# One transformer block on one core: the second gate row made in half 0, residual and gates returned in pieces in half 1, four more raw tiles in the f32 stage

## The chip, the cores and the metric

The kernel runs on one core of a Trainium2 chip. The metric is the device time in microseconds (us). The kernel before was timed three times: 2090.99 us in the median, 2086.14 to 2091.57.

## What is computed

One block over 256 tokens of width 2048, all in f32. The condition `c` gives six rows of 2048 through a matrix `ada_w` of 2048 x 12288. Then follow dilated attention, pooling and an output projection, and the part that matters here, a feed-forward over 16384 experts:

```python
def peer_ffn(xn, w_query, sub_keys, w_down, w_up):     # cut to what matters
    s = ...                                            # scores of 8 heads x 2 x 128 keys
    top_s, top_i = lax.top_k(s, 16)                    # 16 experts of each head and token, with gates
    ...
    u = jnp.take(w_down, ic, axis=0)
    a = jax.nn.gelu(jnp.einsum('cd,ced->ce', xc, u)) * gc
    return jnp.einsum('ce,ced->cd', a, jnp.take(w_up, ic, axis=0))

xn2 = rms_norm(h, norm2_g) * (1.0 + scale2) + shift2
h = h + gate2 * peer_ffn(xn2, ...)
return rms_norm(h, final_g)
```

`gate2` is the sixth of the rows that come from `ada_w`: rows 80 to 95 of its 96 blocks of 128.

## The kernel before, in words

The program is one list of steps, run in order. A step reads one block of weights, 128 x 2048 f32 (1 MiB), as two half blocks of 512 KB (`HW` = 1024 columns), and multiplies it on TensorE. For 192 of the 256 tokens the experts are computed densely: all 16384 rows of `w_down` in 128 blocks, then `w_up`, with the gates as a matrix that is zero for experts not chosen. The blocks are taken in two halves of 64 (`HB`): down layer of half 0, up layer of half 0, down layer of half 1, up layer of half 1. For the other 64 tokens the chosen rows are gathered by POOL's indirect DMAs, 1 MiB each, 128 of them in all (`gather`, `sparse_step`); each gathered tile is multiplied on VectorE. How many of these a step gets stands in a list of shares (L1259): 0.95 of one in the f32 stage from its step 24 on, 0.47 in the up layer of half 0, 0.42 and 0.55 in half 1.

The down layer of half 0 is the f32 stage: its matmuls take raw f32 weights and activations. All other layers split each half block into a rounded high part `hi` (ScalarE, L166) and the rest `lo` (VectorE, L172), four tiles of each, and run the matmuls with both. In these layers a step prepares the splits that are needed one and a half steps later.

Loads. SyncE issues all weight loads in one order (`want`, `fill`, L125). A load goes into one of five raw tiles (`RAW_BUFS`); when all are in use, into a `spare` place if there is one. `take` gives out the oldest load, `give` frees its place and issues the next. The list `spare` is filled with three pieces of hT in the up layer of half 0 and late in half 1 (`room`, L1265), as hT isn't needed then. In the f32 stage it is empty.

Work beside the steps. Up to step 19 of the f32 stage a step also loads one half row of `ada_w` and reduces it on VectorE (`ada_half`, L217): these are the 32 halves of gate2's rows. Generators in `side` issue a piece at each half of a step: `route` (choice of experts and gates), `gate_groups` (24 groups of eight tokens: one-hot tiles on VectorE, gate products on TensorE, L1051; the second half's gates are stored to DRAM as `g2d`, 128 x 24 x 64 x 8), and `residual`. A step's `tick` is called once at its end.

For half 1 the gates come back from `g2d` in four tiles `A` of 21, 21, 21 and 1 blocks (`load_gates`, L1015). The first three are 2 MB each in runs of 672 bytes; the fourth, 96 KB, lies in the tail of hT. They are issued in the up layer of half 0 at its steps 22 and 43, and in half 1 at steps 0 and 24. The tensor h, which waits in DRAM as `hsp`, is brought back into hT (2 MB) by one load at step 1 of half 1 (L1275). `residual` (L1214) is started at step 4: POOL adds up rows 80 to 95 of `mod` (`ada_fix`), writes them as one row `g2row` to DRAM in 4-byte elements, and reads it back as `g2b`, broadcast over 128 partitions (L1218, L1220). Two steps later it transposes hT on TensorE (L1228), four 128 x 128 blocks at a time, eight times, and VectorE makes acc = acc x g2b + h (L1231, L1232); for the second token tile ScalarE also copies 64 rows (L1234). POOL also issues all gathers, in the same queue.

Of the kernel before, what the change touches and what calls it, by code (L numbers as in the profile page):

```python
# [10 lines left out]
F32 = mybir.dt.float32  # L11
F32R = mybir.dt.float32r
U32 = mybir.dt.uint32
AF = mybir.ActivationFunctionType
# [3 lines left out]
P = 128  # L18
D = 2048
S = 256  # L20
KC = D // P
# [6 lines left out]
HB = NB // 2  # L28
SP = 64
ND = S - SP  # L30
AB = 21
RS = 24
TG = 8
HW = 1024
RAW_BUFS = 5
HL_BUFS = 4
# [57 lines left out]
def peer_block_kernel(ctx: ExitStack, tc, xT_d, c_d, cols_d, const_d, ada_d, gates_d, wide_d, blk_d, mix_d, br_d,  # L94
                      wout_d, wq_d, keys_d, down_d, up_d, rows_d, fg_d, out_d):
    nc = tc.nc
# [5 lines left out]
    per = ext(tc.tile_pool(name="per", bufs=1))  # L102
    wst = ext(tc.tile_pool(name="wst", bufs=3))
# [16 lines left out]
    spare, next_spare = [], [0]  # L120
# [84 lines left out]
    hT = per.tile([P, KC, S], F32, name="hT")  # L205
    x2f = hT.rearrange("p k s -> p (k s)")[:, :KC * ND].rearrange("p (k n) -> p k n", n=ND)
    cb = per.tile([P, D], F32, tag="cb", name="cb")
# [36 lines left out]


    class Step:
        def __init__(self, src, mm, evac=None, w=D, ada=(), before=(), after=(), tick=None, exact=False):
            self.exact = exact
            self.src, self.mm, self.evac, self.w = src, mm, evac, w
            self.ada, self.before, self.after, self.tick = list(ada), list(before), list(after), tick  # L250
            self.hs, self.ls = [], []
            self.rows = 0

    steps = []
    side, side2, score_q = deque(), deque(), []
# [45 lines left out]
    def run():  # L301
        for n, parts in plan():
            acts = parts[0] + parts[1]
            if n >= 0 and steps[n].exact:
                acts[:0] = [("half", steps[n], i) for i in range(2)]
            for a in acts:
                if a[0] == "ada":
                    want(ada_d[a[1]][:, a[2] * HW:(a[2] + 1) * HW], HW)
                elif a[0] == "half" and (a[2] == 0 or a[1].w == D):
                    w = min(a[1].w, HW)  # L310
                    want(a[1].src[:, a[2] * w:a[2] * w + w], w)
        want(fg_d.unsqueeze(0).to_broadcast([P, D]))
        for n, parts in plan():
            s = steps[n] if n >= 0 else None
            if n >= 1:
                first = parts[0][0] if parts[0] else None
                if first and first[0] == "half" and not (s and s.exact):
                    parts[0][0] = first + (split_hi(first[1], first[2]),)
                if steps[n - 1].evac:
                    steps[n - 1].evac()  # L320
            if s:
                s.mm(s.hs, s.ls, 0)
                side_step(0)
                s.mm(s.hs, s.ls, 1)
                s.hs, s.ls = None, None
            for a in parts[0]:
                act(a)
            while late:
                late.popleft()()
            for _ in range(s.rows if s else 0):  # L330
                sparse_step()
            if s:
                side_step(1)
                if s.tick:
                    s.tick()
            for a in parts[1]:
                act(a)
        if steps[-1].evac:
            steps[-1].evac()
# [157 lines left out]
    n0 = len(steps)  # L497
# [10 lines left out]
    n0 = len(steps)  # L508
# [235 lines left out]
    while gates:  # L744
        steps.append(branch_step(new.popleft() if new[0] <= have and len(new) >= len(old) else old.popleft()))
        if (len(new) + len(old)) % 2 or len(new) + len(old) < 4:
            c, g = gates.popleft()
# [5 lines left out]
    def table(func):  # L753

        t = pp["st"] if "st" in pp else pa.tile([P, 4], F32, tag="st", name="tb")
        nc.scalar.activation(t[:, 0:1], ones[:, 0:1], func)

    hsp = hdram.tile([P, KC, S], F32, name="hsp")
# [28 lines left out]
    w0 = len(steps)  # L787
    for c in range(KC):
        steps.append(block_step(wout_d[c], lambda k: mgd[k // 8][:, k % 8],
                                lambda ps, c=c: wo_done(c, ps)))  # L790
# [9 lines left out]
        while len(order) - len(todo) < seen * len(order) // total:  # L800
            t.ada.append(todo.popleft())

    steps[w0 + 2].tick = lambda: table(AF.Sqrt)

    def fix_mods():
        ada_fix(32, 48)
# [191 lines left out]
    NG = ND // TG  # L998
    half_state = [dict(A=[], evac=0, g=0), dict(A=[], evac=0, g=NG)]

    gdram = ext(tc.tile_pool(name="gdram", bufs=1, space=bass.MemoryType.DRAM))
    g2d = gdram.tile([P, NG, HB, TG], F32, name="g2d")
    NA = -(-HB // AB)

    def get_A(hs, q):
        while len(hs["A"]) <= q:
            n = min(AB, HB - AB * len(hs["A"]))
            if n == AB:
                hs["A"].append(b16([P, NG, n, TG], F32, "A"))
            else:  # L1010
                tail = hT.rearrange("p k s -> p (k s)")[:, KC * ND:KC * ND + NG * n * TG]
                hs["A"].append(tail.rearrange("p (g n u) -> p g n u", n=n, u=TG))
        return hs["A"][q]

    def load_gates(q):  # L1015

        a = get_A(half_state[1], q)
        nc.sync.dma_start(a, g2d[:, :, q * AB:q * AB + a.shape[2], :])

    def gate_groups():  # L1020
        hs = half_state[0]
# [52 lines left out]
    def h_done(half, bl, ps):  # L1074
        hs = half_state[half]
        dst = get_A(hs, bl // AB)[:, :, bl % AB, :]
        n = hs["g"]
        if n:
            hsum = pp["pk2"].tile([P, NG, TG], F32, tag="s1", bufs=S1_BUFS, name="hsum")
            src = hsum  # L1080
            if half:
                both_halves(ps, hsum.rearrange("p g u -> p (g u)"))
            else:
                src = ps[:, :ND].rearrange("p (g u) -> p g u", u=TG)
            nc.scalar.activation(hsum, src, AF.Gelu)  # L1085
            if n < NG:
                nc.scalar.copy(dst[:, n:], hsum[:, n:])
            late.append(lambda: nc.vector.tensor_mul(dst[:, :n], hsum[:, :n], dst[:, :n]))
        else:
            nc.scalar.activation(dst, ps[:, :ND].rearrange("p (g u) -> p g u", u=TG), AF.Gelu)  # L1090
        hs["evac"] = bl + 1

    def open_late():
        pa_ctx.close()
# [102 lines left out]
    fin = {}  # L1197
# [13 lines left out]
            evacuate(fin["acc"][:, 0, c], oc[2 * q], q)  # L1211
            fold(fin["acc"][:SP, 1, c], oc[2 * q + 1])

    def residual():  # L1214

        ada_fix(80, 96)
        row = gdram.tile([KC, P], F32, name="g2row")
        nc.gpsimd.dma_start(row.rearrange("k p -> p k"), mod[:, 80:96])  # L1218
        g2b = fin["g2b"] = per.tile([P, D], F32, tag="cb", name="g2b")
        nc.gpsimd.dma_start(g2b, row.rearrange("k p -> (k p)").unsqueeze(0).to_broadcast([P, D]))  # L1220
        for _ in range(4):
            yield
        for t in range(2):
            for q in range(4):
                acc = fin["acc"][:, t, q * 512:(q + 1) * 512]
                pt = psum("hpt")
                for i in range(4):
                    nc.tensor.transpose(pt[:, i * P:(i + 1) * P], hT[:, 4 * q + i, t * P:(t + 1) * P], ident)  # L1228
                yield
                n = SP if t else P  # L1230
                nc.vector.tensor_mul(acc[:n], acc[:n], g2b[:n, q * 512:(q + 1) * 512])  # L1231
                nc.vector.tensor_add(acc[:n], acc[:n], pt[:n])  # L1232
                if t:
                    nc.scalar.copy(acc[SP:], pt[SP:])  # L1234
                yield

    for half in range(2):
        n0 = len(steps)
        for bl in range(HB):
            steps.append(block_step(down_d[half * HB + bl], x2act if half else lambda k: x2f[:, k, :],  # L1240
                                    lambda ps, half=half, bl=bl: h_done(half, bl, ps), both=half == 1, exact=half == 0))
        if half == 0:
            for m in range(2 * KC):
                steps[n0 - 12 + m].ada.append((80 + m // 2, m % 2))
            steps[n0 + 2].tick = open_late

            steps[n0 + 5].tick = lambda: side.append(gate_groups())
        oc = []
        for bl in range(HB):
            steps.append(up_step(half, bl, oc))  # L1250
            if half == 0 and bl % AB == 1 and bl > AB:
                steps[-1].tick = lambda q=bl // AB - 1: load_gates(q)
        if half == 0:
            steps[-1].evac = lambda oc=oc: keep(oc)
    steps[n0].tick = lambda: load_gates(NA - 2)
    steps[n0 + 24].tick = lambda: load_gates(NA - 1)


    share = [0.95] * (HB - RS) + [0.47] * HB + [0.42] * HB + [0.55] * (HB - 4)  # L1259
    total, seen = sum(share), 0.0  # L1260
    for i, w in enumerate(share):
        n = int(seen / total * 2 * NP + 1e-6)
        seen += w
        steps[n0 - 2 * HB + RS + i].rows = int(seen / total * 2 * NP + 1e-6) - n
    def room(on):  # L1265

        spare.clear()
        if on:
            f = hT.rearrange("p k s -> p (k s)")
            spare.extend(f[:, i * HW:(i + 1) * HW] for i in range(KC * ND // HW))  # L1270

    steps[n0 - HB + 1].tick = lambda: room(True)
    steps[n0 - 8].tick = lambda: room(False)
    steps[n0 + 26].tick = lambda: room(True)
    steps[n0 + 1].tick = lambda: nc.sync.dma_start(hT, hsp)  # L1275
    steps[n0 + 4].tick = lambda: side.append(residual())
    run()


    pk, pk2 = pp["pk"], pp["pk2"]  # L1280
    small = pk.tile([P, 2, 8], F32, name="small")
    acc, g2b = fin["acc"], fin["g2b"]
    fgb = [take() for _ in range(D // HW)]
    nc.scalar.activation(small[:, 0, 7:8], ones[:, 0:1], AF.Sqrt)
    for t in (1, 0):
        for q in range(4):
            c = slice(q * 512, (q + 1) * 512)
            tmp = b16([P, 512], F32, "fin")
            src = oc[2 * q + t]
            if t:  # L1290
                src = fin["rows"][:, c]
# [7 lines left out]
        for q in range(4):  # L1299
            c = slice(q * 512, (q + 1) * 512)  # L1300
# [72 lines left out]
```

## Time and profile before

| what | us |
|---|---|
| median of three runs | 2090.99 |
| the profiled execution's own time | 2092.7 |
| its span | 2090.8 |
| TensorE busy | 1986.3 |
| VectorE busy | 1682.5 |
| ScalarE busy | 904.2 |
| POOL busy | 378.7 |

The span is the time from the first to the last instruction. TensorE is busy for 95% of it, and 65% of the chain that ended last are its instructions; loads are 12% and VectorE 8%. Matmuls overlap, so the sum of their durations says nothing; busy time and counts do.

### The profile page before, as it was taken

To read this page: it belongs to the slowest core of one execution; us is meant where nothing else is said; L and a number is where in the kernel's file an instruction comes from. 1 tells how busy PE (TensorE), PEld (TensorE's weight loads), DVE (VectorE), ACT (ScalarE), POOL (GpSimd) and SP (SyncE) were. 2 spreads that over 40 slices of the span, in tenths; PEclk is the share of its full clock that TensorE was granted. 3 is DMA by queue.
4 is the path that set the end of the run, shared out by engine and by line. 5 is a ranking of instruction groups with operands and counts; after the bars stand their busy time and mean duration, and the time that the engine had idled before them with its cause. 6 is when DMAs were issued, how large, how long until landed. Compare 5 with 4: busy or idle time off the path is not lost.

```text
span 2090.8 us, 33335 instructions
## 1 busy us (share of the span) xinstructions
PE 1986.3 (95%) x12444; PEld 1836.5 (88%) x12444; DVE 1682.5 (80%) x2908; ACT 904.2 (43%) x1473; POOL 378.7 (18%) x384
## 2 busy tenths in 40 slices
PE   6899999999999998999999999998789999999994
PEld 5788999999999998899998888887689999888883
DVE  8987788889888976478886888876678888888886
ACT  3344554544545511012213554544355555545553
POOL 2201231112115700011111010011111112222220
PEclk8999999999999999999999999999799999999997
DMA  9997877788997777699999999989779998999992
GB/s 368 384 342 255 309 266 263 262 286 304 315 327 245 247 244 243 228 355 373 351 353 367 371 330 359 359 333 323 227 264 332 341 334 316 365 348 354 348 349 75
DMA packets 171971, 648.81 MB, mean 310 GB/s; under 512 B 21025, under 2 KB 30529, under 8 KB 155041
## 3 DMA queue, kind: packets, MB, share of 16 engines
q1 hardware_dynamic: 147568, 499.18, 67.3%
q0 software_dynamic: 19200, 136.87, 17.8%
q10 hardware_dynamic: 5042, 10.64, 1.3%
q8 instruction: 98, 1.61, 0.3%
q14 instruction: 63, 0.52, 0.1%
HBM read 636.13 MB, written 10.49 MB: 309 GB/s over the span
## 4 chain that ended last, share of the span: by engine, by line
PE 65%; DMA 12%; DVE 8%; issue 3%; ACT 2%; POOL 0%; DVEq 0%; ACTq 0%; SPq 0%; POOLq 0%
PE oc L1134 11%; PE oc L1132 11%; PE blk L353 10%; PE blk L189 7%; PE oc L1136 6%; DMA raw<-in_ada_dram 4%; PE blk L183 4%; PE blk L184 4%; PE blk L182 4%; PE blk L190 3%; DVE lo L172 2%; DMA raw<-in_wout_dram 2%; DVE raw L219 2%; PE gps L1051 2%; DMA raw<-in_down_dram 2%
## 5 line engine op out<-in xcount | busy, mean ns | idle before, releaser
L172 DVE TENSOR_TENSOR lo<-raw,hi 128x1024 fp32r<-128x1024 f32 (+1 forms) x484 | 575.0, 1196 | 126.1 <-ACT hi L166 122.6
L166 ACT CAST hi<-raw 128x1024 fp32r<-128x1024 f32 (+1 forms) x484 | 491.2, 1021 | 414.6 <-PE oc L1132 128.6
L353 PE MATMUL blk<-hT,raw 128*128 128x192 f32 x2048 | 344.3, 329 | 12.9 <-DMA raw<-in_down_dram 12.9
L353 PEld LDWEIGHTS blk<-hT,raw 128*128 128x128 f32 x2048 | 335.1, 192 | 16.7 <-issue 11.8
L189 PE MATMUL blk<-xn,hi 128*128 128x384 f32 x1024 | 300.0, 365 | 9.5 <-ACT hi L166 8.9
L190 PE MATMUL blk<-xn,lo 128*128 128x192 f32 x1024 | 260.1, 254 | 18.0 <-DVE lo L172 17.9
L219 DVE SCALAR_TENSOR_TENSOR raw<-raw,cb 128x1024 f32<-128x1024 f32 x165 | 213.5, 1312 | 45.9 <-DMA raw<-in_ada_dram 45.3
L1169 POOL DMA_INDIRECT rows<-in_up_dram,spidx x64 | 126.7, 1979 | 512.5 <-DVE rows L1187 253.7
L190 PEld LDWEIGHTS blk<-xn,lo 128*128 128x128 f32 x1024 | 198.9, 194 | 20.7 <-DVE lo L172 20.7
L189 PEld LDWEIGHTS blk<-xn,hi 128*128 128x128 f32 x1024 | 195.6, 191 | 10.8 <-ACT hi L166 9.5
L1132 PE MATMUL oc<-hi,a 128*128 128x512 f32 x512 | 202.6, 396 | 1.7 <-ACT hsum L1085 1.7
L1134 PE MATMUL oc<-hi,a 128*128 128x512 f32 x512 | 202.7, 396 | 0.0
L1134 PE MATMUL oc<-lo,a 128*128 128x512 f32 x512 | 202.5, 396 | 0.0
L1132 PE MATMUL oc<-lo,a 128*128 128x512 f32 x512 | 202.5, 396 | 0.0
L1136 PE MATMUL oc<-hi,a 128*128 128x512 f32 x512 | 202.5, 395 | 0.0
L166 ACT CAST hi<-hT 128x1024 fp32r<-128x1024 f32 x118 | 124.1, 1052 | 122.9 <-PE oc L1132 72.1
L172 DVE TENSOR_TENSOR lo<-hT,hi 128x1024 fp32r<-128x1024 f32 x118 | 142.8, 1223 | 33.6 <-ACT hi L166 30.7
L1180 DVE SCALAR_TENSOR_TENSOR rows<-rows,rows 128x2048 f32<-128x2048 f32 x64 | 146.2, 2284 | 27.9 <-DMA rows<-in_rows_dram,spidx 27.8
L1169 POOL DMA_INDIRECT rows<-in_rows_dram,spidx x64 | 62.7, 980 | 561.5 <-DVE a L1116 233.6
L1187 DVE SCALAR_TENSOR_TENSOR rows<-rows,sph,rows 128x2048 f32<-128x2048 f32 x63 | 147.8, 2345 | 0.8 <-DMA rows<-in_up_dram,spidx 0.8
L182 PE MATMUL blk<-xna,hi 128*128 128x256 f32 x480 | 139.3, 290 | 0.0
L184 PE MATMUL blk<-xna,lo 128*128 128x256 f32 x480 | 136.3, 284 | 0.0
(298 smaller groups left out, 3990.7 us busy)
## 6 DMA issues: line engine op xcount, KB each, us to landing
raw<-in_down_dram SPq DMA_DIRECT2D x229, 512.0 KB, 6.7
raw<-in_ada_dram SPq DMA_DIRECT2D x165, 512.0 KB, 5.7
raw<-in_up_dram SPq DMA_DIRECT2D x165, 512.0 KB, 6.9
hT<-in_up_dram SPq DMA_DIRECT2D x91, 512.0 KB, 7.2
raw<-in_blk_dram SPq DMA_DIRECT2D x80, 512.0 KB, 5.8
raw<-in_wout_dram SPq DMA_DIRECT2D x32, 512.0 KB, 6.1
raw<-in_wq_dram SPq DMA_DIRECT2D x32, 512.0 KB, 5.6
xraw<-in_ada_dram SPq DMA_DIRECT2D x27, 512.0 KB, 6.4
```

Source lines behind the costliest of these rows:

```text
L166: nc.scalar.copy(hi, r)
L172: nc.vector.tensor_sub(lo, r, s.hs[i].bitcast(F32))
L182: nc.tensor.matmul(out, wh, ah, start=start, stop=False)
L184: nc.tensor.matmul(out, wl, ah, start=False, stop=stop)
L189: nc.tensor.matmul(ps[:, :2 * ND], wh, a.rearrange("p s n -> p (s n)"), start=start, stop=False)
L190: nc.tensor.matmul(ps[:, :ND], wl, a[:, 0, :], start=False, stop=stop)
L219: nc.vector.scalar_tensor_tensor(raw, raw, 1.0, cb[:, i * HW:(i + 1) * HW], op0=ALU.mult, op1=ALU.mult, accum_out=modp[:, i, m:m + 1])
L353: nc.tensor.matmul(st["ps"][:, :ND], raw[:, c], a, start=k == 0, stop=k == KC - 1)
L1132: nc.tensor.matmul(o, a[:, P:P + 2 * SP], w, start=st_, stop=sp_)
L1134: nc.tensor.matmul(o, a[:, :P], w, start=st_, stop=sp_)
L1136: nc.tensor.matmul(o, a[:, P + 2 * SP:], w, start=False, stop=False)
L1169: nc.gpsimd.indirect_dma_start(rows[:, j % 2, :], None, table_rows["down" if j < NP else "up"], bass.IndirectOffsetOnAxis(sp["idx"][:, j % ...
```

## The change

- A step may have several ticks; `tick` becomes a list `ticks`.
- `load_gates` spreads a load over four steps, a quarter of the 24 groups in each (one piece for the small fourth tile). The first two begin where they were. The third begins at step 18 of half 1 instead of step 0.
- hT comes back in four loads at steps 2, 4, 6 and 8 instead of one at step 1; `residual` starts at step 10 instead of 4, without its waits and without the gate row.
- `gate_row`, the POOL part of `residual`, is called at step 22 of the f32 stage.
- At step 1 of the f32 stage `spare` is filled with four new tiles of the `hi` ring, which has no splits in it during that stage, and emptied eight steps before the stage's end.

```diff
-    def load_gates(q):
-        a = get_A(half_state[1], q)
-        nc.sync.dma_start(a, g2d[:, :, q * AB:q * AB + a.shape[2], :])
+    def load_gates(n, q, parts=4):
+        def load(g):
+            a = get_A(half_state[1], q)
+            nc.sync.dma_start(a[:, g], g2d[:, g, q * AB:q * AB + a.shape[2], :])
+        for i in range(parts):
+            g = slice(i * NG // parts, (i + 1) * NG // parts)
+            steps[n + i].ticks.append(lambda g=g: load(g))
...
+    def room(where=None):
+        spare.clear()
+        if where == "h":
+            f = hT.rearrange("p k s -> p (k s)")
+            spare.extend(f[:, i * HW:(i + 1) * HW] for i in range(KC * ND // HW))
+        elif where:
+            spare.extend(wst.tile([P, HW], F32, tag="hi", bufs=HL_BUFS, name="spare") for _ in range(HL_BUFS))
...
-    def residual():
+    def gate_row():
         ada_fix(80, 96)
         row = gdram.tile([KC, P], F32, name="g2row")
         nc.gpsimd.dma_start(row.rearrange("k p -> p k"), mod[:, 80:96])
-        g2b = fin["g2b"] = per.tile([P, D], F32, tag="cb", name="g2b")
-        nc.gpsimd.dma_start(g2b, row.rearrange("k p -> (k p)").unsqueeze(0).to_broadcast([P, D]))
-        for _ in range(4):
-            yield
+        fin["g2b"] = per.tile([P, D], F32, tag="cb", name="g2b")
+        nc.gpsimd.dma_start(fin["g2b"], row.rearrange("k p -> (k p)").unsqueeze(0).to_broadcast([P, D]))
+
+    def residual():
+        g2b = fin["g2b"]
+        yield
...
+            steps[n0 + 1].ticks.append(lambda: room("split"))
+            steps[n0 + 22].ticks.append(gate_row)
+            steps[n0 + HB - 8].ticks.append(lambda: room())
...
-    steps[n0].tick = lambda: load_gates(NA - 2)
-    steps[n0 + 24].tick = lambda: load_gates(NA - 1)
+    for q in range(NA - 2):
+        load_gates(n0 - HB + AB * (q + 1) + 1, q)
+    load_gates(n0 + 18, NA - 2)
+    load_gates(n0 + 24, NA - 1, 1)
...
-    steps[n0 + 1].tick = lambda: nc.sync.dma_start(hT, hsp)
-    steps[n0 + 4].tick = lambda: side.append(residual())
+    for q in range(4):
+        steps[n0 + 2 + 2 * q].ticks.append(lambda c=slice(4 * q, 4 * q + 4): nc.sync.dma_start(hT[:, c, :], hsp[:, c, :]))
+    steps[n0 + 10].ticks.append(lambda: side.append(residual()))
```

## Rows read from the trace of the kernel before

**Rows 1.** Windows by stage: length, busy time and count by engine, clock, DMA share, GB/s.

```profile
core 0: us, PE busy (x) PEld busy (x) DVE busy (x) ACT busy (x) POOL busy (x), PEclk, DMA share, GB/s
...
725.00:1131.00 406.00, 392.70 (x2518) 388.54 (x2517) 289.85 (x900) 72.75 (x293) 42.70 (x46) 0.99 0.87 310
1131.00:1432.00 301.00, 298.62 (x1280) 239.79 (x1278) 243.17 (x315) 153.02 (x196) 32.84 (x31) 1.00 0.94 348
1432.00:1763.00 331.00, 304.19 (x2077) 300.64 (x2078) 257.34 (x306) 171.48 (x264) 44.38 (x31) 0.95 0.88 307
```

**Rows 2.** Chain of waits in the f32 stage: start us, us, what.

```profile
926.75 1.78 PE gps L1051 x16
928.54 7.80 PE blk L353 x48
```

**Rows 3.** Windows of the two stretches and of half 1's rest.

```profile
744.00:858.00 114.00, 101.11 (x584) 97.23 (x583) 74.08 (x316) 12.54 (x28) 1.14 (x2) 0.97 0.74 245
...
1432.00:1615.00 183.00, 156.19 (x1036) 152.64 (x1037) 130.67 (x156) 85.29 (x132) 20.79 (x17) 0.92 0.84 284
1615.00:1763.00 148.00, 148.00 (x1043) 148.00 (x1042) 126.67 (x151) 86.19 (x132) 23.59 (x14) 1.00 0.91 335
```

**Rows 4.** Chain of waits, 765 to 810 us.

```profile
776.59 4.38 DMA raw<-in_ada_dram
...
781.00 1.25 DVE raw L219 x2
...
782.26 6.17 DMA raw<-in_ada_dram
```

**Rows 5.** SyncE's waits, 733 to 858 us: us in total, times, longest.

```profile
SPq L141 <- DVE raw L219: 41.8, 8, 6.7
...
SPq L141 <- PE blk L353: 9.0, 7, 2.8
```

**Rows 6.** Timeline of SyncE's issues at the start of half 1.

```profile
1437.81 0.75 SPq L1018 DMA_DIRECT2D A<-g2d  x1
...
1445.76 0.43 SPq L1275 DMA_DIRECT2D hT<-hsp  x1
```

**Rows 7.** ScalarE's waits, 1432 to 1600 us.

```profile
ACT hi L166 <- DMA raw<-in_down_dram: 25.6, 5, 8.0
```

**Rows 8.** Timeline of POOL, 1465 to 1500 us; idle time before in brackets.

```profile
1470.52 1.25 POOL L1218 DMA_DIRECT2D g2row<-mod  x1 [0.29 <-POOL mod L227]
1485.02 0.57 POOL L1220 DMA_DIRECT2D g2b<-g2row  x1 [13.26 <-DMA g2row<-mod]
```

**Rows 9.** VectorE's waits, 1432 to 1600 us.

```profile
DVE acc L1231 <- DMA g2b<-g2row: 17.0, 1, 17.0
```

**Rows 10.** Windows of single stretches of half 1, columns as in rows 1.

```profile
1505.00:1520.00 15.00, 15.00 (x109) 14.78 (x107) 12.97 (x17) 5.99 (x10) 2.31 (x2) 1.00 0.81 266
1442.00:1447.00 5.00, 5.00 (x37) 5.00 (x36) 4.39 (x5) 1.99 (x4) 0.10 (x1) 1.00 1.05 323
...
1448.00:1464.00 16.00, 10.28 (x67) 9.39 (x65) 3.66 (x6) 4.14 (x8) 0.58 (x1) 0.91 1.01 410
...
1475.00:1487.00 12.00, 8.82 (x61) 8.18 (x59) 3.07 (x5) 2.06 (x3) 1.57 (x2) 0.92 0.99 121
```

**Rows 11.** Chain of waits, 893 to 910 us: the first gather.

```profile
883.16 10.42 DMA rows<-in_rows_dram,spidx
```

**Rows 12.** Timeline of VectorE in the residual's second token tile.

```profile
1519.58 1.23 DVE L172 TENSOR_TENSOR lo<-raw,hi 128x1024 fp32r<-128x1024 f32 x1 [1.72 <-ACT hi L166]
...
1522.55 0.68 DVE L1231 TENSOR_TENSOR acc<-acc,g2b 64x512 f32<-64x512 f32 x1
...
1531.87 1.23 DVE L172 TENSOR_TENSOR lo<-raw,hi 128x1024 fp32r<-128x1024 f32 x1 [1.72 <-ACT hi L166]
...
1540.28 1.23 DVE L172 TENSOR_TENSOR lo<-raw,hi 128x1024 fp32r<-128x1024 f32 x1 [1.72 <-ACT hi L166]
```

**Rows 13.** Window around the fourth gate load.

```profile
1600.00:1615.00 15.00, 14.23 (x98) 13.72 (x98) 12.56 (x14) 9.91 (x15) 1.68 (x1) 1.00 1.01 390
```

More of the change, by code (lines that the diff above doesn't have):

```diff
@@ L246, in peer_block_kernel, with __init__ @@
     class Step:
-        def __init__(self, src, mm, evac=None, w=D, ada=(), before=(), after=(), tick=None, exact=False):
+        def __init__(self, src, mm, evac=None, w=D, ada=(), before=(), after=(), exact=False):
             self.exact = exact
             self.src, self.mm, self.evac, self.w = src, mm, evac, w
-            self.ada, self.before, self.after, self.tick = list(ada), list(before), list(after), tick
+            self.ada, self.before, self.after = list(ada), list(before), list(after)
             self.hs, self.ls = [], []
-            self.rows = 0
+            self.rows, self.ticks = 0, []
     steps = []
@@ L333, in run @@
                 side_step(1)
-                if s.tick:
-                    s.tick()
+                for f in s.ticks:
+                    f()
             for a in parts[1]:
@@ L801, in peer_block_kernel @@
             t.ada.append(todo.popleft())
-    steps[w0 + 2].tick = lambda: table(AF.Sqrt)
+    steps[w0 + 2].ticks.append(lambda: table(AF.Sqrt))
     def fix_mods():
@@ L1244, in peer_block_kernel @@
                 steps[n0 - 12 + m].ada.append((80 + m // 2, m % 2))
-            steps[n0 + 2].tick = open_late
-            steps[n0 + 5].tick = lambda: side.append(gate_groups())
+            steps[n0 + 1].ticks.append(lambda: room("split"))
+            steps[n0 + 2].ticks.append(open_late)
+            steps[n0 + 5].ticks.append(lambda: side.append(gate_groups()))
+            steps[n0 + 22].ticks.append(gate_row)
+            steps[n0 + HB - 8].ticks.append(lambda: room())
         oc = []
@@ L1250, in peer_block_kernel @@
             steps.append(up_step(half, bl, oc))
-            if half == 0 and bl % AB == 1 and bl > AB:
-                steps[-1].tick = lambda q=bl // AB - 1: load_gates(q)
         if half == 0:
             steps[-1].evac = lambda oc=oc: keep(oc)
-    steps[n0].tick = lambda: load_gates(NA - 2)
-    steps[n0 + 24].tick = lambda: load_gates(NA - 1)
+    for q in range(NA - 2):
+        load_gates(n0 - HB + AB * (q + 1) + 1, q)
+    load_gates(n0 + 18, NA - 2)
+    load_gates(n0 + 24, NA - 1, 1)
     share = [0.95] * (HB - RS) + [0.47] * HB + [0.42] * HB + [0.55] * (HB - 4)
@@ L1264, in peer_block_kernel @@
         steps[n0 - 2 * HB + RS + i].rows = int(seen / total * 2 * NP + 1e-6) - n
[L1265 to L1274, printed above, removed]
-    steps[n0 + 1].tick = lambda: nc.sync.dma_start(hT, hsp)
-    steps[n0 + 4].tick = lambda: side.append(residual())
+    steps[n0 - HB + 1].ticks.append(lambda: room("h"))
+    steps[n0 - 8].ticks.append(lambda: room())
+    steps[n0 + 26].ticks.append(lambda: room("h"))
+    for q in range(4):
+        steps[n0 + 2 + 2 * q].ticks.append(lambda c=slice(4 * q, 4 * q + 4): nc.sync.dma_start(hT[:, c, :], hsp[:, c, :]))
+    steps[n0 + 10].ticks.append(lambda: side.append(residual()))
     run()
```

## The prediction, made before the changed kernel was run

> **What bounds the kernel now.** I read the stages first. The reader is to see that TensorE is busy all but 2 us of the up layer of half 0 [rows 1]: nothing hidden there is worth anything. The losses lie in the two down layers. A step of either is 32 matmuls. In the f32 stage an undisturbed step is 32 x 7.80/48 = 5.20 us, and after every step and a half 16 small gate products add 1.78 [rows 2]. From 744 to 858 us, its steps 2 to 19, TensorE ran 584 matmuls, 3 of them transposes: 581 x 0.1625 = 94.4 us of work in 114, so 19.3 us were lost [rows 3]. In half 1's down layer the undisturbed rate is 148/1043 = 0.1419 us a matmul, 4.54 us a step. From 1432 to 1615 us there are 1036, of which 32 are the residual's transposes: 1004 x 0.1419 = 142.5 in 183, an excess of 40.5 us [rows 3]. These two stretches are what the change touches; together they are 59.8 us.
>
> Next I read what each stretch waits for. In the first, the chain is load, VectorE, load: an `ada` half row lands in 4.38 to 6.17 us, VectorE multiplies it in 1.25, and only then the next `ada` load starts [rows 4]. SyncE, which issues all loads in order, waited mostly for VectorE there (41.8 us for that multiplication alone) and 9.0 for TensorE [rows 5]: the five raw tiles are shared out so that one goes round among the `ada` rows, and the weight loads stand behind it. In the second stretch two things are seen. The 2 MB of gates and the 2 MB of hT were issued 8 us apart [rows 6], ahead of the weights, and ScalarE waited 25.6 us for raw tiles [rows 7]. Then the gate row: its write to DRAM held POOL 13.26 us before the broadcast could be issued [rows 8], and VectorE stood 17.0 us at the first residual product [rows 9] with the splits queued behind it. In both stretches the granted clock fell (0.97 and 0.92 in the mean, 1.00 beside them [rows 3]), so part of each excess is matmuls at 1.2 GHz after a stall; it goes with the stalls.
>
> **The f32 stage: four more raw tiles.** Nothing is added but 2 MB fetched earlier. Nine loads are three steps, so an `ada` load waits for a multiplication about three steps back and no longer for the last one. The DMA need is 1.5 MiB a step, 1.573 MB; at the 410 GB/s of a saturated stretch [rows 10] that is 3.84 us of 5.20. VectorE's 74.1 us of work in the stretch [rows 3] have to fit in 94.7: they do, at 78%. So I expect steps near 5.2 us from about step 4 on. At best all 19.3 us go; at worst none, if the `ada` chain stays (a rival). I take 17, near the best, since the floor is held right after step 19, where the `ada` loads end. The first two steps keep their loss, because the tiles are opened at the end of step 1.
>
> **The gate row in half 0.** Its POOL work goes from half 1 to step 22 of the f32 stage: two small adds, the row's write 1.25, a wait of 13.26, the broadcast 0.57, some 16 us [rows 8]. POOL had 1.14 us to do in that stretch [rows 3], and its queue doesn't wait for TensorE, so it starts when the last `ada` product (step 19) is made: about 858 - 17 = 841 in the new time, done at 857. Queued behind it are the first two row gathers, then due at 883 - 17 = 866 [rows 11]: 9 us to spare. The row's write also clogs the DMA engines: from 1475 to 1487 they were 0.99 busy and moved 121 GB/s [rows 10]. In the new place there are no `ada` loads any more and nine tiles hold 4.5 steps, 23 us of weights, against 12. I cost it at nothing; without that cover it is the 12 us of the clog or the 13.26 of POOL.
>
> **Gates in quarters in the up layer.** No step there lost anything with 2 MB in one piece [rows 1], so quarters bring and cost nothing.
>
> **The start of half 1.** The gates' 2 MB leave steps 0 to 8; hT comes in four pieces at steps 2, 4, 6, 8; the 17.0 us wait for the row is gone, as the row has been there since half 0. What is late next is the DMA. A step needs 1 MiB of weights (2.56 us at 410 GB/s [rows 10]), 0.42 of a 1 MiB gather (the share in the code; 1.07 us), and half a piece of hT (0.64): 4.27 us of 4.54. It fits, barely. I take 1 us, between 0 and 3.
>
> **The residual at steps 11 to 18.** Its 32 transposes stay: 109 matmuls took 15.00 us, 12 of them transposes [rows 10], so (15.00 - 97 x 0.1419)/12 = 0.10 each, 3.3 us. Its VectorE work is a product of 0.68 us a step [rows 12] and a sum that I take to be as long, and for the second token tile a ScalarE copy waits for VectorE and the splits stand behind that copy. Before, such steps took 6.1 us, and 8.4 with a gathered row (12.29 us for two, 8.41 for the next [rows 12]); 20.70 for three, against 4.96 with transposes. But there VectorE came out of the 17 us wait with no split ready ahead. With splits one and a half steps ahead I expect most of it hidden: 2 us, between 0 and 4 x (6.90 - 4.96) = 7.8.
>
> **The third gate tile at steps 18 to 21.** A quarter runs at 323 GB/s [rows 10], 1.62 us: the step's DMA need is 2.56 + 1.07 + 1.62 = 5.25, 0.7 too much, 2.8 in four steps, partly covered by the raw tiles: 2 us, between 0 and 5.7 (twice 2.8, if the residual has left no lead). Here a rule speaks against the change. The Trainium skill, "DMA: Bandwidth & Descriptors", section "Rules for kernel authors", wants at least 1 MiB per DMA, and its section on the anatomy of one DMA gives a fixed cost of about 2.0 us each. If these costs stood one behind the other, an estimate by that page for the 12 additional DMAs would be 24 us, and the sum would give back half of what it gains. The up layer moved 348 GB/s in loads of 512 KB with its DMA engines 0.94 busy [rows 1]; so the trace does not agree that pieces of this size are slow when others are queued behind them.
>
> The small fourth gate load at step 24 is unchanged; what it costs lies in the last 15 us, 15.00 - 98 x 0.1419 = 1.1 [rows 13].
>
> **The sum.** Half 1: of 40.5, there remain 3.3 + 1.1 + 1 + 2 + 2 = 9.4; 31.1 go. With 17 of the f32 stage 48.1. The profiled execution took 2092.7 us (span 2090.8), so 2044.6; it was 1.7 above the median of the runs shown, so **2043 us** for a median.
>
> **Rivals.**
> 1. The f32 stage gains nothing: raw tiles come round so that each `ada` load still waits for the last multiplication. For it: that is how five tiles behaved, against the number of tiles. Against: the four new tiles go round in a fixed order, three steps apart. 2060.
> 2. Half 1 keeps its pace: VectorE and ScalarE wait for each other in the residual (7.8), hT costs 3, the third gate tile 5.7. For it: the 8.41 us came with ScalarE as the releaser and not a load [rows 12]. There remain 20.9: 2054.5.
> 3. The gate row is late or clogs the loads in the f32 stage: up to 13.3 more, 2056. For it: 9 us to spare is not much.
> 4. Slower: in half 1 steps 2 to 21 the DMA queue saturates with only five raw tiles, and each step takes the 8.41 us of the slowest residual step. 20 x (8.41 - 4.54) = 77.4, and 1.1, in the place of 40.5; with the 17 us of the f32 stage 2091 - 17 + 38 = 2112. It decides when a step's DMA need passes 4.54 us for all twenty; by my working it is 4.27, and 5.25 only in four.
> 5. The pieces cost their whole latency: 12 more DMAs, each holding the loads behind it for 4.38 us as one `ada` load did [rows 4], are 53 us: 2096, no change. Against: the up layer's rate [rows 1]. That is what the rule above would come to here.
>
> **Chances.** Forecast 0.60, rival 1 0.14, rival 2 0.14, rival 3 0.06, rival 4 0.03, rival 5 0.03. The likeliest case alone spans 2036 (both stretches at their best: 19.3 and 36.1) to 2050. The range reaches to rivals 1, 2 and 3, and below by half of the spread of the runs shown: 2033 to 2063. A measurement of this kernel tells 0.3%, 6 us, from no change: faster 0.94, same 0.03, slower 0.03.
>
> **What will show it.** f32 stage: steps 2 to 19 should take 95 to 97 us, VectorE's wait for `ada` loads should shrink and SyncE should wait for TensorE; an unchanged 114 is rival 1. The write of the row should start near 841 us and the gathers not move against their picks; an idle TensorE before the gate products is rival 3. Half 1: no VectorE wait for the row, and 1432 to 1615 shrunk to about 152 us; steps over 6 us from the eleventh to the eighteenth are rival 2, ScalarE waiting for raw tiles from step 2 on is rival 4. The up layers must stay as they are. I am wrong if either stretch gives back less than half.

## The result, and the profile after

The changed kernel took 2041.0 us in the median of four runs (2039.94 to 2044.54); beside it the kernel before took 2091.28. The ratio is 0.976, with a 95% interval of 0.974 to 0.979: some 50 us less. It was run again later on another chip: 2041.9 against 2092.5, ratio 0.9755 (0.974 to 0.977). The forecast was 2043.

The stages of the profiled execution (2039.94 us, span 2038.1), in the columns of [rows 1]:

```profile
726.00:1112.00 386.00, 386.00 (x2522) 385.94 (x2521) 290.17 (x904) 73.47 (x293) 45.45 (x51) 1.00 0.92 328
1112.00:1413.00 301.00, 298.93 (x1281) 240.02 (x1279) 243.81 (x317) 152.67 (x195) 33.75 (x31) 1.00 0.94 348
1413.00:1712.00 299.00, 296.71 (x2082) 295.39 (x2083) 257.85 (x306) 172.67 (x266) 44.70 (x27) 1.00 0.93 338
```

Against [rows 1] the f32 stage went from 406 to 386 us, the up layer stayed at 301, half 1's down layer went from 331 to 299: 52 us, of 52.8 between the two profiled executions (50 between the medians: the one profiled here was the fastest of its four). TensorE is now busy for all of the f32 stage, and the granted clock is 1.00 in all three.

Steps 2 to 19 of the f32 stage, which took 114 us before, and then the same 114 us of the trace as in [rows 3], which now reach into step 23:

```profile
746.00:840.00 94.00, 94.00 (x582) 93.98 (x581) 78.36 (x331) 12.30 (x27) 2.79 (x5) 1.00 0.92 317
744.00:858.00 114.00, 114.00 (x704) 113.98 (x703) 87.42 (x362) 13.62 (x31) 3.34 (x6) 1.00 0.92 302
```

704 matmuls where there were 584, none waiting. The DMA engines are at 0.92 instead of 0.74. What SyncE waits for, 734 to 840 us, has changed sides against [rows 5], and the chain there, which was loads and VectorE [rows 4], is TensorE alone:

```profile
SPq L141 <- PE blk L353: 67.5, 35, 2.8
SPq L141 <- DVE tops L860: 7.7, 2, 6.0
```

```profile
764.92 25.19 PE blk L353 x155
```

POOL's timeline, against [rows 8] and [rows 11]:

```profile
834.36 0.22 POOL L226 TENSOR_TENSOR mod<-modp 128x16 f32<-128x16 f32 x1 [82.46 <-DVE spare L219]
...
835.17 1.21 POOL L1231 DMA_DIRECT2D g2row<-mod  x1 [0.29 <-POOL mod L227]
849.40 0.55 POOL L1233 DMA_DIRECT2D g2b<-g2row  x1 [13.03 <-DMA g2row<-mod]
865.24 1.03 POOL L1183 DMA_INDIRECT rows<-in_rows_dram,spidx  x1 [15.29 <-DVE spidx L1176]
```

The write still holds POOL 13.03 us, but the first gather comes 15 us after the broadcast and waits for its own indices, not for POOL's queue. The clog is still there too and costs nothing: from 835 to 850 the DMA engines are 0.90 busy with 164 GB/s, and TensorE runs through. In half 1, the start with hT's pieces, the residual, and the stretch with the last two gate tiles:

```profile
835.00:850.00 15.00, 15.00 (x94) 15.00 (x93) 13.40 (x42) 0.82 (x3) 1.76 (x2) 1.00 0.90 164
1423.00:1460.00 37.00, 37.00 (x263) 37.00 (x262) 30.66 (x35) 21.73 (x33) 5.03 (x3) 1.00 0.97 368
1460.00:1500.00 40.00, 40.00 (x289) 40.00 (x289) 37.40 (x47) 20.96 (x34) 6.71 (x4) 1.00 0.82 295
1500.00:1560.00 60.00, 58.18 (x403) 56.91 (x401) 50.53 (x62) 34.20 (x53) 8.39 (x5) 1.00 0.99 355
1600.00:1700.00 100.00, 100.00 (x705) 100.00 (x705) 84.30 (x98) 58.11 (x89) 15.45 (x9) 1.00 0.90 326
```

Under hT's pieces the DMA engines are 0.97 busy and TensorE loses nothing. Only the fourth line loses: 60.00 - 403 x 0.1419 = 2.8 us. VectorE, which stood 17.0 us for the gate row [rows 9], doesn't wait for it any more. Its waits in steps 0 to 38 are short ones, nearly all for ScalarE's copies of sums:

```profile
DVE hsum L195 <- ACT hsum L194: 19.2, 17, 2.3
```

### The profile page after: what moved, and what is told of

Same layout as the page of the kernel before. It is cut to its first block, busy times and chain, and to the rows that moved or that the text cites. A ratio compares the mean times of both kernels' runs of the same rounds, so it can differ in the third digit from the quotient of the medians.

```text
span 2038.1 us, 33369 instructions
## 1 busy us (share of the span) xinstructions
PE 1973.6 (97%) x12444; PEld 1828.1 (90%) x12444; DVE 1683.2 (83%) x2908; ACT 905.6 (44%) x1473; POOL 387.6 (19%) x384
## 4 chain that ended last, share of the span: by engine, by line
PE 74%; DVE 7%; DMA 6%; ACT 2%; issue 2%; DVEq 0%; ACTq 0%; POOL 0%
PE blk L353 16%; PE oc L1146 12%; PE oc L1148 12%; PE blk L189 8%; PE oc L1150 6%; PE blk L183 4%; PE blk L182 4%; PE blk L184 4%; PE blk L190 4%; DVE lo L172 2%; DMA raw<-in_wout_dram 2%; DMA raw<-in_blk_dram 2%; PE gps L1056 2%; DVE raw L219 1%; ACT hi L166 1%
## 5 line engine op out<-in xcount | busy, mean ns | idle before, releaser
L189 PE MATMUL blk<-xn,hi 128*128 128x384 f32 x1024 | 293.2, 360 | 0.7 <-ACT acc L551 0.7
L1183 POOL DMA_INDIRECT rows<-in_up_dram,spidx x64 | 141.4, 2209 | 480.7 <-DVE rows L1201 241.7
L353 PE MATMUL blk<-hT,raw 128*128 128x192 f32 x1280 | 212.3, 326 | 0.0
L353 PEld LDWEIGHTS blk<-hT,raw 128*128 128x128 f32 x1280 | 207.7, 190 | 0.0
L219 DVE SCALAR_TENSOR_TENSOR raw<-raw,cb 128x1024 f32<-128x1024 f32 x153 | 197.5, 1311 | 9.5 <-DMA raw<-in_ada_dram 9.5
```

The lines of the kernel that those rows point to most:

```text
L189: nc.tensor.matmul(ps[:, :2 * ND], wh, a.rearrange("p s n -> p (s n)"), start=start, stop=False)
L219: nc.vector.scalar_tensor_tensor(raw, raw, 1.0, cb[:, i * HW:(i + 1) * HW], op0=ALU.mult, op1=ALU.mult, accum_out=modp[:, i, m:m + 1])
L353: nc.tensor.matmul(st["ps"][:, :ND], raw[:, c], a, start=k == 0, stop=k == KC - 1)
L1183: nc.gpsimd.indirect_dma_start(rows[:, j % 2, :], None, table_rows["down" if j < NP else "up"], bass.IndirectOffsetOnAxis(sp["idx"][:, j % ...
```

## The experiments

Each kernel is the changed one with one part altered, or the kernel before with one part of the change. Times are medians beside runs of the kernel before on the same chip; "lost" is the length of a stretch less its matmuls at 0.1625 us (f32 stage) or 0.1419 (half 1) and less 0.1 us for each transpose, where any are taken off. The "clog" is the stretch in which the row's write is under way and the DMA engines move little; the "lead" is what splits are ready ahead of TensorE. In these traces the f32 stage's first matmul starts between 729.5 and 735.7 us, though no edit touches what runs before it; so differences of a few us between kernels are better read from the windows than from the medians.

**1. Without the four extra raw tiles.**

```diff
-            steps[n0 + 1].ticks.append(lambda: room("split"))
```

> The changed kernel without the four extra raw tiles in the f32 stage (five tiles throughout it), all else kept. Theory: those tiles alone took the 19.3 us out of steps 2 to 19, so about 19 us come back: 2060. The gate row's write now falls on five tiles instead of nine: where I costed it at nothing under the cover of nine tiles, up to 12 us more should show as TensorE waiting for weight loads in steps 20 to 23: 2060 to 2072, I expect about 2065. Rival: the gain of the f32 stage came from elsewhere (the load order, the moved row): 2041 to 2045.

2062.8 us, ratio 0.986 (0.984 to 0.988): 22 us of the gain gone. The window of steps 2 to 19 and of the gate row's write, and SyncE's waits before 858 us:

```profile
745.00:859.00 114.00, 103.50 (x613) 100.36 (x612) 79.99 (x335) 12.65 (x28) 2.79 (x5) 0.99 0.79 258
859.00:877.00 18.00, 15.82 (x97) 15.35 (x96) 7.49 (x24) 0.99 (x3) 0.55 (x1) 1.00 0.98 218
```

```profile
SPq L141 <- DVE raw L219: 36.4, 8, 7.1
...
SPq L141 <- PE blk L353: 16.1, 14, 2.8
```

SyncE waits for VectorE again, 114.0 - 0.3 - 610 x 0.1625 = 14.6 us are lost, and the clog costs 18.0 - 97 x 0.1625 = 2.2 more: far from 12. Of the 19.5 us between the profiled executions of this kernel and the changed one, the other 3 or so are in half 1, which ran at the slower of two rhythms (last section). So the time came out near the expected one, but the stretch itself gave back 14.6 us and not 19: with five tiles its loss was 19.3 before, 14.6 here and 17.0 in experiment 5, and why it varies isn't shown. The rival falls.

**2. One extra tile instead of four**, to tell the `ada` chain from the depth of the queue.

```diff
-            spare.extend(wst.tile([P, HW], F32, tag="hi", bufs=HL_BUFS, name="spare") for _ in range(HL_BUFS))
+            spare.extend(wst.tile([P, HW], F32, tag="hi", bufs=HL_BUFS, name="spare") for _ in range(1))
```

> The changed kernel with one extra raw tile in the f32 stage instead of four (six tiles), all else kept. Chain theory: the five tiles let each ada load wait for the ada product just before it; with six, the ada rows alternate between the sixth tile and others, so a load waits for a product two steps back, and most of the 19 us stays gained: at most 5 us are lost again, 2041 to 2046, and SyncE waits for TensorE, not for VectorE. Depth theory (the rival): what counts is how many loads are ahead, each tile giving its share: one of four keeps a quarter, so 12 to 15 us come back: 2053 to 2058.

2043.7 us, ratio 0.978 (0.975 to 0.981). Steps 2 to 19, and the row's write behind them; SyncE's waits, 734 to 850 us; and three `ada` loads with two of the products:

```profile
741.00:835.00 94.00, 94.00 (x581) 93.98 (x580) 74.48 (x319) 12.21 (x27) 2.40 (x5) 1.00 0.90 303
835.00:860.00 25.00, 22.72 (x130) 22.45 (x129) 12.45 (x39) 1.32 (x4) 0.93 (x2) 0.93 0.88 242
```

```profile
SPq L141 <- PE blk L353: 61.4, 32, 4.8
SPq L141 <- DVE raw L219: 9.1, 4, 4.3
```

```profile
746.49 0.33 SPq L141 DMA_DIRECT2D raw<-in_ada_dram  x1
...
752.07 0.42 SPq L141 DMA_DIRECT2D spare<-in_ada_dram  x1
...
756.89 0.33 SPq L141 DMA_DIRECT2D raw<-in_ada_dram  x1
```

```profile
754.61 1.21 DVE L219 SCALAR_TENSOR_TENSOR raw<-raw,cb 128x1024 f32<-128x1024 f32 x1
...
759.72 1.22 DVE L219 SCALAR_TENSOR_TENSOR spare<-spare,cb 128x1024 f32<-128x1024 f32 x1
```

The 581 matmuls of [rows 3] take 94.00 us with six tiles as with nine (582 in the changed kernel, 581 in experiment 3). The `ada` rows alternate between a raw tile and the sixth: the load at 756.89 goes out 2.8 us before the product of the row ahead of it begins, where with five tiles it started as that product ended [rows 4]. So one tile more, which parts successive `ada` rows, takes all of that loss away: the chain theory holds, and depth at so much a tile does not. The other three tiles matter behind it: with six, the clog costs 25.0 - 130 x 0.1625 = 3.9 us.

**3. The four tiles alone, in the kernel before.**

```diff
+    def split_room():
+        spare.extend(wst.tile([P, HW], F32, tag="hi", bufs=HL_BUFS, name="spare") for _ in range(HL_BUFS))
...
+            steps[n0 + 1].tick = split_room
...
+            steps[n0 + HB - 8].tick = spare.clear
```

> The kernel before with the four extra raw tiles in the f32 stage and nothing else. Theory: it gains what its removal cost by the matmul count of steps 2 to 19, 18 to 20 us: 2071 to 2073, with half 1 as it was (its steps 4 to 16 with some 40 us of excess). Rival: faster arrival at half 1 or other buffers change half 1 too: outside 2068 to 2076.

2076.0 us, ratio 0.993 (0.990 to 0.995), at the edge of the rival's bound. The trace says why:

```profile
743.00:837.00 94.00, 94.00 (x581) 93.82 (x580) 78.29 (x331) 12.21 (x27) 1.14 (x2) 1.00 0.92 318
```

```profile
1431.00:1614.00 183.00, 156.37 (x1034) 153.16 (x1033) 132.34 (x158) 86.73 (x134) 22.21 (x17) 0.92 0.85 287
1614.00:1742.00 128.00, 128.00 (x885) 128.00 (x884) 107.54 (x126) 72.79 (x111) 20.20 (x12) 1.00 0.89 324
```

All of the f32 stage's loss is gone, and half 1's first 183 us are as in [rows 3] (1034 matmuls, 1036 before). But the rest of half 1 ran at 128/885 = 0.1446 us a matmul instead of 0.1419, 2.4 us here, of which the last section tells.

**4. The gate row made in half 1 again.**

```diff
-            steps[n0 + 22].ticks.append(gate_row)
...
     def residual():
+        gate_row()
         g2b = fin["g2b"]
-        yield
+        for _ in range(4):
+            yield
```

> The changed kernel with the gate row made again at the start of the residual in half 1 (step 10 there, transposes four half steps later, as before), all else kept. Theory: the row's clog of the DMA engines and VectorE's wait for the broadcast are the larger part of half 1's gain: VectorE again waits 10 to 17 us at the first residual product and 15 to 22 us come back: 2056 to 2063. Rival: the wait of 17 us was itself a consequence of the two 2 MB loads, which delayed the row; with these in pieces the row's chain takes its 13 + 10 us mostly beside other work: 2041 to 2047.

2059.9 us, ratio 0.984 (0.982 to 0.986): 19 us back, with hT and the gates in pieces. VectorE's wait, POOL's wait for the row, and the window from there to the residual's end:

```profile
DVE acc L1249 <- DMA g2b<-g2row: 7.1, 1, 7.1
```

```profile
1480.29 0.57 POOL L1233 DMA_DIRECT2D g2b<-g2row  x1 [13.30 <-DMA g2row<-mod]
```

```profile
1474.00:1546.00 72.00, 59.46 (x387) 57.28 (x387) 50.95 (x64) 31.57 (x49) 6.70 (x6) 0.93 0.86 267
```

The time came as expected, the wait did not: 7.1 us instead of 10 to 17. So the rival was right in part: from write to arrival the row took 24 us in both kernels, but in the kernel before VectorE stood at it for 10 us longer. Lost are 72.0 - 3.3 - 355 x 0.1419 = 18.3 us, so more than half of it lies outside that wait, in the clog and in the steps after the wait, which have no lead; the two weren't told apart.

**5. The row early, alone, in the kernel before.**

```diff
-    def residual():
+    def gate_row():
...
+    def residual():
+
+        g2b = fin["g2b"]
...
+            steps[n0 + 22].tick = gate_row
```

`gate_row` is what `residual` did ahead of its yields.

> The kernel before with the gate row made at step 22 of the f32 stage and nothing else; residual still starts at step 4 of half 1, hT and the third gate tile still come in one load each at steps 1 and 0. Theory: VectorE's 17 us wait goes and with it the slow residual steps behind it; the 4 MB of loads still cost their 10 us; the row's clog under five raw tiles costs about 3 in the f32 stage: 2068 to 2076. Rival: with the row there early VectorE waits in the same place for something else (the gathers, the raw tiles behind the 4 MB), and half of the 17 us stays: 2078 to 2086.

2081.5 us, ratio 0.996 (0.994 to 0.998): 11 us, a miss, within the rival's bounds. The 4 MB of loads, then the residual:

```profile
1454.00:1477.00 23.00, 16.62 (x98) 15.74 (x98) 13.09 (x17) 10.06 (x16) 1.68 (x1) 0.85 0.85 329
...
1502.00:1541.00 39.00, 33.34 (x207) 32.10 (x207) 31.44 (x38) 19.13 (x29) 3.95 (x3) 0.91 0.71 237
859.00:879.00 20.00, 17.32 (x97) 17.05 (x96) 12.25 (x38) 0.80 (x4) 0.75 (x2) 0.91 0.94 223
```

VectorE doesn't wait for the row any more, but 23.0 - 98 x 0.1419 = 9.1 us are lost to the loads, and the residual, close behind, goes at the slow pace of [rows 12]: 39.0 - 207 x 0.1419 = 9.6 us, 12 transposes included. The likely reason is that the loads use up the lead. The clog on five tiles costs 4.2 in the f32 stage. So the parts aren't additive: the row's 19 us are to be had in full only with the loads out of the residual's way and more tiles under the row.

**6. hT and the third gate tile early and whole again.**

```diff
-    load_gates(n0 + 18, NA - 2)
+    load_gates(n0, NA - 2, 1)
...
-    for q in range(4):
-        steps[n0 + 2 + 2 * q].ticks.append(...)
+    steps[n0 + 1].ticks.append(lambda: nc.sync.dma_start(hT, hsp))
```

> The changed kernel with the third gate tile in one load at step 0 and hT in one load at step 1 of half 1, as before, the gate row still in half 0 and the residual still at step 10. Theory: the 4 MB ahead of five raw tiles cost steps 4 to 8 what they cost before, 8 to 12 us: 2049 to 2053. Rival: with no row and no residual close behind them the loads are made up by the lead of the splits: 2041 to 2044.

2051.6 us, ratio 0.981 (0.979 to 0.983). The window of these loads, and ScalarE's wait for raw tiles in half 1 (16.0 us in the changed kernel, 5.2 of them before 1500 us, where TensorE lost nothing):

```profile
1422.00:1455.00 33.00, 26.47 (x164) 25.67 (x164) 20.64 (x24) 12.94 (x21) 5.03 (x3) 0.90 0.91 347
```

```profile
ACT hi L166 <- DMA raw<-in_down_dram: 31.3, 13, 7.7
```

33.0 - 164 x 0.1419 = 9.7 us lost, as in the theory; the rival falls. From step 21 on this trace, too, has the slower rhythm of the last section.

**7. The new places, but whole loads.**

```diff
-    def load_gates(n, q, parts=4):
+    def load_gates(n, q, parts=1):
...
-    for q in range(4):
-        steps[n0 + 2 + 2 * q].ticks.append(...)
+    steps[n0 + 2].ticks.append(lambda: nc.sync.dma_start(hT, hsp))
```

> The changed kernel with each of the three 2 MB gate loads and hT in one piece, at the places where their pieces begin now (up layer steps 22 and 43; half 1 step 18 for gates, step 2 for hT). Theory: where eight tiles are there (the up layer) nothing changes; in half 1 each 2 MB load ahead of five raw tiles stalls TensorE for 3 to 6 us, so 2046 to 2053. By the rule that pieces cost a fixed time each it would be faster than with pieces: below 2041.

2043.9 us, ratio 0.9765 (0.9745 to 0.978): a miss on the low side, by its median not told from the changed kernel. hT's 2 MB in one load at step 2 stalled nothing (steps 2 to 10 took 4.55 us each); the last two gate tiles did. Both together, then the third alone:

```profile
1501.00:1553.00 52.00, 48.36 (x321) 47.14 (x320) 39.35 (x47) 26.58 (x43) 6.72 (x4) 0.97 0.94 325
1514.00:1530.00 16.00, 14.03 (x86) 13.55 (x86) 11.77 (x13) 8.77 (x14) 1.68 (x1) 0.89 0.88 318
```

52.0 - 321 x 0.1419 = 6.5 us, 3.8 of it for the third tile, against 2.8 for both tiles with the third in quarters (5.5 in the second trace of the changed kernel). So 2 MB in one load cost nothing for hT and 3.8 us for a gate tile, and the two issued 8 us apart ahead of five tiles cost 9 to 10. It isn't the size alone; but the gate tile by itself at step 0 wasn't run, so how much of the 10 us is its own stays open. Nor is the reverse true: whole loads are not faster.

**8. The last two gate tiles later still.** Twice; the second time beside the changed kernel on one chip.

```diff
-    load_gates(n0 + 18, NA - 2)
-    load_gates(n0 + 24, NA - 1, 1)
+    load_gates(n0 + 24, NA - 2)
+    load_gates(n0 + 32, NA - 1)
...
-    steps[n0 + 26].ticks.append(lambda: room("h"))
+    steps[n0 + 20].ticks.append(lambda: room("h"))
```

> The changed kernel with hT's three extra raw tiles opened at step 20 of half 1 instead of 26, the third gate tile in quarters at steps 24 to 27 instead of 18 to 21, and the small fourth tile in quarters at steps 32 to 35 instead of whole at 24. The changed kernel still loses about 3.3 us over its step of 4.55 at steps 19, 20, 25, 29 and 30. Theory: with eight raw tiles these loads are covered as in the up layer: up to 3 us faster, 2038 to 2041. Rival: the small runs of 32 bytes cost the DMA engines the same wherever they stand: 2041.

> The changed kernel itself once more, beside the next one on one chip. Both theories: 2041.

> The kernel with the last two gate tiles later, under eight raw tiles, again. Theory: the 3.3 us of stalls at steps 19, 20, 25, 29 and 30 are what it gains, 2.5 of them in the trace: 2036 to 2039, its runs below those of the changed kernel on the same chip. Rival: the 4.6 us between the medians came from different chips and from the part of the program before the change: 2040 to 2042.

2036.4 us, ratio 0.975 (0.972 to 0.977); then 2036.5, ratio 0.974 (0.972 to 0.975), where the changed kernel took 2041.9. On the shared chip its five runs were 2034.9 to 2040.4, those of the changed kernel 2039.1 to 2042.8. The two windows, of this kernel and then of the changed one, from the last pair:

```profile
1500.00:1560.00 60.00, 59.01 (x414) 58.50 (x413) 54.53 (x65) 35.90 (x56) 9.52 (x6) 1.00 0.99 370
1560.00:1700.00 140.00, 140.00 (x987) 140.00 (x986) 118.15 (x137) 81.52 (x124) 20.81 (x14) 1.00 0.93 338
```

```profile
1500.00:1560.00 60.00, 56.15 (x384) 54.62 (x383) 49.33 (x58) 32.99 (x52) 8.39 (x5) 1.00 0.98 348
1560.00:1700.00 140.00, 140.00 (x967) 140.00 (x967) 117.78 (x136) 79.45 (x122) 21.89 (x13) 1.00 0.90 330
```

1.3 us lost in the first 60 where the changed kernel lost 5.5, and 20 matmuls more in the next 140 us, 2.8 us. The first is what the theory said; the second is the slower rhythm of the last section, which this trace of the changed kernel has, its first trace doesn't, and neither trace of this kernel does. It is the version with the lowest median; the intervals of the two ratios overlap and so do the runs, the medians on the shared chip are 5.4 us apart, and the windows account for 7. Three things moved at once (the tiles opened earlier, the third gate tile later, the fourth later and in quarters), and which of them does it wasn't told apart.

## Why the prediction was right

- **f32 stage, 17 us.** The stage shrank by 20. The mechanism held as put: the `ada` chain through one tile (experiments 1 and 2), with more tiles than it needs, since one parts the rows. VectorE's wait for `ada` loads fell from 42.6 us to 18.6, as the signs asked. The term was sized too small: all of the 19.3 went, and some 0.7 of step 27 that I had not counted.
- **Gate row in half 0 at no cost.** It held; the write began at 835 us (841 forecast), the first gather at 865 (866). The price without cover was put too high: 12 us by the clog's length, 2.2 to 4.2 with five tiles and 3.9 with six, since even these hold part of it.
- **Quarters in the up layer.** Nothing, as said.
- **hT in pieces, 1 us.** Nothing was lost. The DMA need of 4.27 us of 4.54 is 0.94, and 0.97 busy was measured; but the pieces weren't needed, as one piece at the same place did as well (7). The sign of rival 4, ScalarE waiting for raw tiles, did show (16.0 us), without reaching TensorE under hT's pieces.
- **Residual, 3.3 for transposes and 2.** 289 matmuls took 40.00 us; with 28 transposes, 261 x 0.1419 = 37.0, so 0.11 a transpose (0.10 forecast), and nothing else lost. That the splits' lead hides this work fits the two runs in which a stall just before had used it up and the slow pace came back (4 and 5). It isn't shown by itself: no run has the residual at step 4 with the rest of the change.
- **Last two gate tiles, 2 and 1.1.** 2.8 in the profiled execution, 5.5 in the second: within the 0 to 5.7 given for the third tile and 1.1 for the fourth.
- **The rule on large loads** (the Trainium skill, "DMA: Bandwidth & Descriptors", "Rules for kernel authors") would, by the prediction's estimate, have given 24 us back. The fixed cost in that estimate is one that the Trainium skill, on the same page in "Anatomy of one DMA", gives for DMAs issued by GpSimd; these loads are issued by SyncE. No run here shows such a cost. With loads of 512 KB the DMA engines moved 368 GB/s at 0.97 busy, and whole 2 MB loads gained nothing (7).
- **The sum.** 31.1 forecast for half 1, 32 measured; 48.1 in all, 52 measured in the profiled executions and 50 by the medians. No error cancels another: the f32 stage gave 3 us more than its term, and the 3 us set aside for hT's pieces and the residual weren't used. The parts lean on each other: taken out one at a time they cost 22, 19 and 11 us, put in alone the first two bring only 16 and 11 (in the profiled executions the slower rhythm has some 3 us of the 22 and of the loads' 11, and both kernels with one part alone have it too).

## What to carry to other kernels

When loads for two consumers share a ring of tiles in one issue order, see which load waits for which consumer: here one tile more parted the slow consumer from the queue, and the further tiles bought only cover for a disturbance. A slow transfer that the end of a chain needs, such as a row written element by element, belongs where buffers are full, and work that leans on a lead must not stand right behind what uses the lead up.

## What was not expected of the hardware

In half 1's down layer the matmuls keep one of two rhythms, at a granted clock of 1.00 and with no wait in the trace: 100/705 = 0.142 us each in the first trace of the changed kernel, 140/967 = 0.145 in its second, 128/885 = 0.145 in experiment 3. The traces of the kernel before, of the changed kernel, of experiment 4 and both of experiment 8 end in the first; the second trace of the changed kernel and experiments 1, 2, 3, 5, 6 and 7 end in the second. A run changes at a step where it was disturbed, most often by the small fourth load, and as a rule keeps the new rhythm to the stage's end; it can also change back (in experiment 2 steps 21 and 22 took 4.64 us each and steps 26 to 28 took 4.55). Over some 33 steps the difference is 3 us, so it is part of what these experiments cost, and it may be part of the spread between runs of one kernel. Its cause stays open.

While the row of 8 KB was written in 4-byte elements the DMA engines were busy and moved little, in both places: 121 GB/s at 0.99 busy over 12 us [rows 10], 164 GB/s at 0.90 over 15 us in its new place, against 317 in steps 2 to 19. That the write is the cause is read from its being there each time; no run leaves it out.
